# Low parts of split weights: a ScalarE copy and an accumulating DMA in place of a VectorE subtraction

## The chip, the cores and the metric

The kernel runs on one core of one Trainium2 chip. The metric is the device time of one execution in microseconds, as the median of the runs; the profile is one execution with its instructions recorded.

## The reference

The reference takes 512 tokens of 1024 features through one hybrid block (a selective state-space branch, a gated linear recurrence, retention and RWKV-7, merged by gates, then a gated feed-forward with a short convolution) and through two layers of a second block (three kinds of attention merged by gates, a feed-forward, a per-layer embedding). All of it is float32. Most of the work is in products of activations with weights, of this kind:

```
proj   = h @ w_in                      # [512, 1024] @ [1024, n]
branch = einsum('bsmw,mwd->bsmd', ys, w_branch)
x      = x + (silu(gate) * value) @ w_down
```

## The kernel before, in words

Activations lie with features on the 128 partitions and the 512 tokens along the free dimension. A product makes one chunk of 128 output features at a time. Its weights come as one tile of 128 partitions by 1024 columns (eight blocks of 128 input features; some have 768, 512, 256 or 128 columns).

TensorE multiplies in a fast format that keeps some 12 bits of an operand. So each operand is held as two parts, high and low, whose sum is the float32 value, and each block of a product is three matmuls: high by high, high weights by low activations, low weights by high activations (`mm3`, L226). `wtile` (L218) brings one weight tile in and splits it: SyncE loads the float32 weights into a tile `wr` (pool of NWR = 3 buffers), ScalarE rounds them into `whi` (3 buffers), and VectorE subtracts `whi` from `wr` into `wlo` (2 buffers). The helper `act` (L164, the instruction at L166) is the ScalarE copy, `tt` (L175, L176) the VectorE subtraction, `dma` (L169, L170) the load on SyncE's queue, `mm` (L172, L173) the matmul. `pmm` (L233) runs the three matmuls of each block into one PSUM tile `pj` (2 buffers), 24 matmuls for a tile of eight blocks. `proj` (L242) is one tile load and its `pmm`. Nearly all weight tiles go through `proj`; values and embeddings call `wtile` themselves (L995, L1197, L1741), and so do the compressed keys and values of attention (`compress`, L1436; its wtile at L1451), whose tiles feed only eight short matmuls each, and which stand between projections of full length.

The program calls `wtile` 579 times. The framework orders the instructions of each engine ahead of time and puts semaphores between engines; an engine works its own list strictly in order. A tile's buffer is written again once the last reader of the tile that held it is done. So the copy into `whi` of one tile waits for the last matmul of the tile three before it, and the load into `wr` waits for the subtraction of the tile three before it. GpSimd has hardly anything to do: it clears tiles and takes the power -0.5 of a few columns for the norms (`rsqrt`, L246, the instruction at L251). No DMA is issued on its queue.

The stages, by time from the start of the span: the RWKV projections and the recurrence up to about 400 us, the state-space and retention branches with the RWKV inverse to about 800, the RWKV scan woven with the branch products to about 1230, the feed-forward to about 1650, then two layers of attention (each some 550 us, with `compress` in the first 50) and feed-forward (each some 450 us).

Of the kernel before, what the change touches and what calls it, by code (L numbers as in the profile page):

```python
# [11 lines left out]
F32R = mybir.dt.float32r  # L12
# [7 lines left out]
P = 128  # L20
# [7 lines left out]
NWR = 3  # L28
# [10 lines left out]
def _param_layout():  # L39
    """Columns of the packed per-feature parameters: name -> (first column, columns)."""  # L40
    sizes = [
        ("norm_mix", 8), ("ssm_conv_w", 64), ("ssm_conv_b", 16), ("ssm_norm", 8), ("ssm_d", 8),
        ("lru_conv_w", 32), ("lru_conv_b", 8), ("lru_b_a", 8), ("lru_b_i", 8), ("lru_lam", 8),
        ("ret_norm", 8), ("rwkv_mu", 26), ("rwkv_w0", 8), ("rwkv_a0", 8), ("rwkv_k_k", 8),
        ("rwkv_k_a", 8), ("rwkv_r_k", 8), ("rwkv_ln_w", 8), ("rwkv_ln_b", 8), ("norm_ffn", 8),
        ("ffn_conv_w", 132), ("ffn_conv_b", 44), ("norm_final", 8),
        ("mix_norm_2", 16), ("ffn_norm_2", 16), ("ple_norm_2", 16), ("c_q_norm_2", 4),
        ("c_kv_norm_2", 4), ("final_norm_2", 8),
    ]
    out, c = {}, 0  # L50
    for n, w in sizes:
        out[n] = (c, w)
        c += w
    return out, c
# [3 lines left out]
# constants that depend on shapes alone: name -> (first column, columns)  # L58
# [15 lines left out]
class Unit:  # L74
    """Softmax attention of 128 queries over T sets of n keys that share a bank of scores."""
# [65 lines left out]
class B:  # L141
    """The parts of the program share these helpers, pools and constants."""
# [66 lines left out]
    def split(self, hi, lo, src, scale=None):  # L209
        """hi + lo == src (times a per-feature column), each part exact in the fast format."""  # L210
# [7 lines left out]
    def wtile(self, src, n=1024):  # L218
        raw = self.wr.tile([P, 1024], F32, tag="wr", name=self.name("wr"))
        self.dma(raw[:, :n], src)  # L220
        hi = self.wh.tile([P, 1024], F32R, tag="whi", name=self.name("whi"))
        lo = self.wh.tile([P, 1024], F32R, tag="wlo", name=self.name("wlo"), bufs=2)
        self.split(hi[:, :n], lo[:, :n], raw[:, :n])
        return hi, lo

    def mm3(self, out, ws, xs, first, last):  # L226
        """out += (wh + wl)^T (xh + xl) without the product of the two low parts."""
# [5 lines left out]
    def pmm(self, w, off, x, kc, m=P):  # L233
        """One chunk of m output features from the split weights w, from column off on."""
# [7 lines left out]
    def proj(self, src, x, kc=KC, m=P):  # L242
        """One chunk of m output features: src is [128, kc * m] of DRAM, x the split activations."""
        return self.pmm(self.wtile(src, kc * m), 0, x, kc, m)

    def rsqrt(self, out, ss, scale, eps):  # L246
        """out = (ss * scale + eps) ** -0.5 on a few columns."""
# [5 lines left out]
    def col_sums(self, out, xs):  # L253
        """out[:, t]: sums of the columns of all xs, tokens on partitions."""
# [6 lines left out]
    def rstd_rows(self, sq, dst, n=D):  # L261
        """sq: [128, S] (or several), whose column sums are sums of squares; dst[:, t] = rsqrt(mean + eps)."""
# [6 lines left out]
    def bcast_cols(self, r, dst):  # L269
        """The columns r [128, 4] of tokens as one row [., S] on every partition."""  # L270
# [9 lines left out]
    def softplus_neg_abs(self, out, ax, tmp):  # L280
        """out = log1p(exp(-ax)) for ax >= 0, by 2 atanh(e / (2 + e))."""
# [24 lines left out]
    def block1_consts(self):  # L306
# [23 lines left out]
        # 4 * softplus(-lam)  # L330
# [14 lines left out]
    def first_norm(self):  # L345
        """h = rms_norm(x) in two parts, features on partitions."""
# [28 lines left out]
    # -- RWKV --  # L375
    def rwkv_setup(self, pool):
# [11 lines left out]
        # w2: high parts on the lower half of the partitions, low parts on the upper; a2 the other way round  # L388
# [12 lines left out]
    def mix(self, pool, ps, ch, tag, bufs):  # L401
        """Token shift: x (1 - mu) + previous x mu."""
# [5 lines left out]
    def rwkv_lora(self, pool):  # L408
        """Chunks 24 (wl | al) and 25 (gl) of the mixed projection."""
# [20 lines left out]
    def lora(self, i, cs):  # L430
        """The second product of decay (0) or rate (1): (high + low) high, then high low."""
# [13 lines left out]
    def rwkv_core(self, pool, p):  # L445
# [6 lines left out]
        # decay  # L452
# [11 lines left out]
        # a  # L464
# [5 lines left out]
        # normalised key direction  # L470
# [19 lines left out]
        # bonus  # L490
# [6 lines left out]
        # values, tokens of a chunk on partitions, the two heads stacked  # L497
# [57 lines left out]
    def swap_halves(self, dst, src):  # L555
        """dst[(h, t), c, v] = src[(h, v), (c, t)] for halves h of the partitions and chunks c of 64."""
# [9 lines left out]
    def rwkv_inverse(self, pool):  # L566
        """(I + A)^-1 of every head and chunk, A strictly upper triangular: forward substitution in the two
        diagonal blocks of 32, one problem a partition, then the block above them by matrix products."""
# [25 lines left out]
        # four problems on the partitions: -X11 (A12 X22), with A12 and then (X11 A12)^T on block diagonals  # L594
# [60 lines left out]
    def rwkv_step(self, pool, p, c, st, ld, bank):  # L655
        """One chunk of the recurrence over the states of a pair of heads."""
# [32 lines left out]
    def rwkv_scan(self, pool, p, y):  # L689
        """The recurrence of a pair of heads, its norm and output."""  # L690
# [38 lines left out]
    # -- RG-LRU --  # L729
    def conv4(self, pool, ps, w, n, ch, b, tag, bufs=2, taps=4):  # L730
        """Causal depthwise convolution along the tokens of [128, S]."""
# [47 lines left out]
    # -- Mamba-2 --  # L779
    def silu_gate(self, pool, ps, tag, tmp, bufs=1):  # L780
        """silu(ps) = (1 + tanh(x / 2)) x / 2."""
# [7 lines left out]
    def ssm_setup(self, pool, tmp):  # L789
        """dt, its cumulative sums about each block's middle, and what follows from them."""  # L790
# [38 lines left out]
        # from the block's start, and about its middle  # L829
# [7 lines left out]
        # dt exp(end - cum)  # L837
# [112 lines left out]
    # -- retention --  # L950
    def rope(self, pool, ps, cos, sin, half, rows, tag, bufs=1, tmp=(("ropr", 1), ("rops", 1))):
        """x cos + swap(x) sin, halves of each head swapped across partitions by DMA."""
# [12 lines left out]
    def stack(self, pool, src, e, tag, bufs=1):  # L965
        """[high; low] parts of head e stacked on the partitions."""
# [6 lines left out]
    def dup(self, pool, src, e, tag, bufs=1):  # L973
        """The high part of head e on both halves of the partitions, and the low part."""
# [9 lines left out]
    def ret_pair(self, pool, j, y):  # L984
# [7 lines left out]
        # values with tokens on partitions  # L992
# [54 lines left out]
    def finish_ret(self):  # L1047
        """The last steps of the heads whose norms were begun one stage before."""
# [8 lines left out]
    # -- gates, branch products, merge --  # L1057
# [4 lines left out]
    def gates1(self, pool):  # L1062
        """tanh(gate / 2) of the four branches, chunk by chunk."""
# [7 lines left out]
    def branch(self, pool, m, y, gates, norm=None):  # L1071
        """merged (+)= (1 + tanh(gate / 2)) * (y_m W_m): twice the gated sum."""
# [20 lines left out]
    def norm_in(self, pool, c, x, w, acc, tag="nsq", bufs=2, gain=1.0):  # L1093
        """Chunk c of x (times gain) joins the sum of squares; its product with w is split into h."""
# [11 lines left out]
    def new_row(self):  # L1106
        """The row of 1 / rms by which products with h are still to be multiplied."""
# [6 lines left out]
    def out_proj(self, pool, w, m, xres, gain, g0, tag="xr", bufs=4, due=None):  # L1114
        """x += m w; the new x goes to DRAM, its normalised form to h. due: a row and gains still missing in x."""
# [15 lines left out]
    def ffn(self, up, down, conv, pool, done, mid=None, late=None):  # L1131
        """x + W_down (silu(gate) value); done(j, x_j) takes each finished chunk."""
# [51 lines left out]
    def embeddings(self, pool, i, tags=None):  # L1184
        """The per-layer embeddings p W of layer i, to DRAM."""
# [22 lines left out]
    def mid_norm(self, pool, fill):  # L1208
        """Block 1's last norm and block 2's first: x still lacks the first one's gain and row1, h the row of both."""
# [19 lines left out]
    def block1(self):  # L1229
# [10 lines left out]
        def weave(main, fill, ratio):  # L1240
            """One step of `fill` after every `ratio` steps of `main`; then what is left of fill."""
# [99 lines left out]
    def rope_tables(self, tmp):  # L1341
        """cos and signed sin of positions x frequencies, the angle reduced to [-pi, pi]."""
# [38 lines left out]
    def rope_load(self, pool, n, row):  # L1381
        """The rotary tables, times the row of 1 / rms if that is still due."""
# [18 lines left out]
    def rope2(self, pool, pt, cs, half, tag="ra", bufs=2):  # L1401
        """x cos + swap(x) sin, halves of each head swapped across partitions by DMA."""
# [16 lines left out]
    def to_tokens(self, pool, src, tag, rows=P, n=P, bufs=1):  # L1419
        """[rows, S] features x tokens to [128 tokens, 4, n]."""  # L1420
# [8 lines left out]
    def compress(self, pool, i, src, kv, out):  # L1429
        """gelu((blocks + pos) w1): leaves the hidden activations' transpose [128, 2, 64] in out."""  # L1430
# [15 lines left out]
        for t in range(4):  # L1446
            # high parts in columns 0 to 63 of each product's stationary operand, low parts in the others
# [24 lines left out]
    def attn_a_setup(self, pool, i):  # L1472
        """Projections of branch A: queries, its three kinds of keys and values, gates."""
# [24 lines left out]
        # selected and window keys side by side, high parts and low parts on both halves  # L1498
# [14 lines left out]
        # compressed keys on both halves of the partitions, one block of columns a head of a pair  # L1513
# [11 lines left out]
        # compressed values, one copy for each head of the group on its own rows and columns  # L1525
# [33 lines left out]
    def units(self, seq):  # L1559
        """Attention units in stages, each unit's transposes and products behind later units' scores."""  # L1560
# [24 lines left out]
    def o_chunk(self, oN, o, c):  # L1585
        """Features 128 c.. of the outputs back to features on partitions, split."""
# [5 lines left out]
    def attn_a(self, pool, o):  # L1592
        """Compressed, selected (every block is among the selected) and window attention."""
# [72 lines left out]
    def attn_b(self, pool, i, o):  # L1666
        """Sliding window of a block of queries over its own and the previous block, with sinks."""
# [27 lines left out]
    def attn_c_setup(self, pool, i):  # L1695
        """Normalised low-rank queries and keys, and the shared rotary key."""
# [38 lines left out]
    def attn_c(self, pool, i, o):  # L1735
        """Latent attention: 64 plain and 32 rotary features a head."""
# [3 lines left out]
        # values, tokens on partitions  # L1740
# [9 lines left out]
        # the rotary key is the same for every head  # L1750
# [48 lines left out]
    def gates2(self, pool, i):  # L1799
        """tanh(gate / 2) of the three branches, chunk by chunk."""  # L1800
# [8 lines left out]
    def branch2(self, pool, i, m, o, gates):  # L1809
        """merged (+)= (1 + tanh(gate / 2)) (o W): twice the gated sum."""  # L1810
# [19 lines left out]
    def weave(self, main, fill, ratio):  # L1830
        """One step of fill after every `ratio` steps of main."""
# [7 lines left out]
    def layer2(self, i, last):  # L1839
# [31 lines left out]
        with tc.tile_pool(name="ff2", bufs=1, reuse_waits="tile") as pool:  # L1871
# [11 lines left out]
            # per-layer embedding  # L1883
# [33 lines left out]
def _ahead(gs):  # L1917
    """The items of gs, each handed out once the next one has been prepared."""
# [188 lines left out]
```

## Time and profile before

| what | value |
|---|---|
| median of 3 runs | 3707.62 us (3706.73 to 3713.56) |
| span of the profiled execution, first to last instruction | 3707.9 us |
| instructions | 47402 |
| granted TensorE clock, mean over the span | 0.988 |

The profile gives no other time of that execution than its span; the span lies 0.3 us above the median and within the spread of the runs, so differences are counted against 3707.9 us and put on the median unchanged. "Busy" counts a TensorE matmul from its start to a modelled end. Consecutive matmuls overlap, so the step from one start to the next is shorter than one matmul's busy time. PEld is the loading of the stationary operand, beside the matmuls.

### The profile page before, as it was taken

What the parts mean: (1) busy time and instruction counts of PE and PEld (TensorE: products, weight loads), DVE (VectorE), ACT (ScalarE), POOL (GpSimd) and SP (SyncE); (2) the same over time, 40 slices, a digit from 0 to 9 for tenths busy, and PEclk for the clock granted to TensorE, in tenths of its full rate; (3) what the DMA queues carried; (4) which work ended last, traced back from release to release, by engine and by line L of the source; (5) the groups of instructions that cost most, each with busy time, mean ns of one, the idle gap of its engine ahead of it and who ended that gap; (6) DMA issues with size and microseconds to landing.
All of it is one profiled execution on the core that took longest, in us unless ns stands there. A gap on an engine that the chain in (4) does not pass through costs nothing.

```text
span 3707.9 us, 47402 instructions
## 1 busy us (share of the span) xinstructions
PE 3630.3 (98%) x17806; PEld 2953.0 (80%) x17806; DVE 2328.7 (63%) x4416; ACT 1543.6 (42%) x2619; POOL 53.2 (1%) x61
## 2 busy tenths in 40 slices
PE   8999999999999999999999999999999999999998
PEld 6887788877878788877888787888778887878886
DVE  6777897654454586657776655544677766554445
ACT  5665533323233353344555533222445655432223
POOL 0000000000000000000000000000000000000000
PEclk9999999999999999999999899999999999999999
DMA  5443545355543532344222124233442221343332
GB/s 182 141 135 116 154 123 142 107 152 161 158 132 108 162 108 91 103 135 150 76 66 68 58 82 154 92 96 95 139 134 80 64 69 55 102 141 96 95 93 97
DMA packets 230388, 417.86 MB, mean 113 GB/s; under 512 B 99632, under 2 KB 105648, under 8 KB 230032
## 3 DMA queue, kind: packets, MB, share of 16 engines
q1 hardware_dynamic: 230160, 414.84, 36.3%
q8 instruction: 141, 2.31, 0.3%
q14 instruction: 87, 0.71, 0.1%
HBM read 349.81 MB, written 55.38 MB: 109 GB/s over the span
## 4 chain that ended last, share of the span: by engine, by line
PE 66%; DVE 2%; ACT 1%; issue 0%; DMA 0%; POOL 0%; SPq 0%; POOLq 0%; DVEq 0%; ACTq 0%
PE pj L173 56%; PE ps L173 4%; PE pl L173 4%; PE ps L119 2%; DVE wlo L176 0%; DVE cc L176 0%; PE ps L1589 0%; POOL r L251 0%; ACT PT L166 0%; DVE ro L176 0%; ACT qf L166 0%; ACT P L167 0%; DVE kd L176 0%; DVE qf L176 0%; DVE xa L193 0%
## 5 line engine op out<-in xcount | busy, mean ns | idle before, releaser
L173 PE MATMUL pj<-hhi,whi 128*128 128x512 f32 (+1 forms) x2824 | 1137.6, 403 | 6.4 <-DVE scv L193 2.1
L173 PE MATMUL pj<-hhi,wlo 128*128 128x512 f32 (+1 forms) x2824 | 1127.2, 399 | 5.9 <-DVE wlo L176 5.8
L173 PE MATMUL pj<-hlo,whi 128*128 128x512 f32 (+1 forms) x2824 | 1128.0, 399 | 0.0
L166 ACT ACTIVATE whi<-wr 128x1024 fp32r<-128x1024 f32 (+3 forms) x579 | 573.4, 990 | 1289.1 <-PE pj L173 1140.3
L176 DVE TENSOR_TENSOR wlo<-wr,whi 128x1024 fp32r<-128x1024 f32 (+3 forms) x579 | 654.8, 1131 | 165.1 <-PE pj L173 104.2
L173 PEld LDWEIGHTS pj<-hhi,wlo 128*128 128x128 f32 (+1 forms) x2824 | 531.4, 188 | 135.9 <-DVE wlo L176 10.3
L173 PEld LDWEIGHTS pj<-hhi,whi 128*128 128x128 f32 (+1 forms) x2824 | 532.1, 188 | 130.8 <-issue 3.3
L173 PEld LDWEIGHTS pj<-hlo,whi 128*128 128x128 f32 (+1 forms) x2824 | 532.2, 188 | 122.8 <-issue 4.5
L173 PE MATMUL pj<-gl,whi 128*128 128x512 f32 x528 | 208.6, 395 | 0.0
L173 PE MATMUL pj<-gh,wlo 128*128 128x512 f32 x528 | 208.6, 395 | 0.0
L173 PE MATMUL pj<-gh,whi 128*128 128x512 f32 x528 | 208.5, 395 | 0.0
L176 DVE TENSOR_TENSOR fg<-pj,row 128x512 f32<-128x512 f32 x82 | 56.7, 691 | 212.7 <-PE pj L173 212.6
L176 DVE TENSOR_TENSOR xa<-pj,xa 128x512 f32<-128x512 f32 x72 | 49.8, 692 | 193.5 <-PE pj L173 193.3
L167 ACT ACTIVATE P<-ps,a 128x256 f32<-128x256 f32 (+3 forms) x256 | 128.3, 504 | 53.8 <-DVE a L189 49.9
L173 PE MATMUL pj<-o,whi 128*128 128x512 f32 x384 | 132.5, 421 | 0.0
L173 PE MATMUL pj<-yh,whi 128*128 128x512 f32 x320 | 131.1, 410 | 1.4 <-ACT yh L166 1.4
L173 PE MATMUL pj<-yl,whi 128*128 128x512 f32 x320 | 129.4, 404 | 0.5 <-DVE yl L176 0.5
L173 PE MATMUL pj<-yh,wlo 128*128 128x512 f32 x320 | 128.9, 403 | 0.0
L166 ACT ACTIVATE PT<-ps 128x256 f32<-128x256 f32 (+3 forms) x200 | 98.3, 492 | 71.0 <-PE ps L119 56.9
L173 PEld LDWEIGHTS pj<-gl,whi 128*128 128x128 f32 x528 | 99.0, 187 | 24.3
L173 PEld LDWEIGHTS pj<-gh,whi 128*128 128x128 f32 x528 | 99.0, 187 | 24.2
L173 PEld LDWEIGHTS pj<-gh,wlo 128*128 128x128 f32 x528 | 99.0, 187 | 24.2
(504 smaller groups left out, 5209.9 us busy)
## 6 DMA issues: line engine op xcount, KB each, us to landing
wr<-in_ffn_up SPq DMA_DIRECT2D x132, 512.0 KB, 3.4
wr<-in_w_in SPq DMA_DIRECT2D x122, 512.0 KB, 3.7
wr<-in_ffn_down SPq DMA_DIRECT2D x48, 512.0 KB, 3.5
wr<-in_w_bg SPq DMA_DIRECT2D x48, 512.0 KB, 3.4
wr<-in_w_gate SPq DMA_DIRECT2D x32, 512.0 KB, 3.5
wr<-in_w_branch SPq DMA_DIRECT2D x32, 512.0 KB, 3.5
wr<-in_w_out SPq DMA_DIRECT2D x24, 512.0 KB, 3.5
wr<-in_w_br SPq DMA_DIRECT2D x48, 256.0 KB, 2.6
```

Source lines behind the costliest of these rows:

```text
L119: b.nc.tensor.transpose(pt[:, k * P:(k + 1) * P], self.P[:, k * P:(k + 1) * P], b.ident)
L166: return self.nc.scalar.activation(out, in_, f, bias=bias, scale=scale)
L167: return self.nc.scalar.activation(out, in_, f, bias=bias, scale=scale, accum_out=accum)
L173: return self.nc.tensor.matmul(out, lhsT, rhs, start=start, stop=stop)
L176: return self.nc.vector.tensor_tensor(out, a, b, op=op)
```

## The change

In `wtile` the split is written out anew. ScalarE writes minus the rounded weights into `wlo` (a copy with scale -1) and then the rounded weights into `whi` as before. A DMA issued on GpSimd's queue then reads the same weights from DRAM a second time and adds them onto `wlo` in place, so that `wlo` ends as weights minus rounded weights. VectorE has no part in it. The raw tile `wr` has 2 buffers in place of 3, `wlo` has 3 in place of 2, `whi` still has 3. The other lines of the diff take out docstrings and comments and leave the instructions as they are; line numbers stay.

```diff
-NWR = 3
+NWR = 2
...
     def wtile(self, src, n=1024):
         raw = self.wr.tile([P, 1024], F32, tag="wr", name=self.name("wr"))
         self.dma(raw[:, :n], src)
-        hi = self.wh.tile([P, 1024], F32R, tag="whi", name=self.name("whi"))
-        lo = self.wh.tile([P, 1024], F32R, tag="wlo", name=self.name("wlo"), bufs=2)
-        self.split(hi[:, :n], lo[:, :n], raw[:, :n])
+        hi = self.wh.tile([P, 1024], F32R, tag="whi", name=self.name("whi"), bufs=3)
+        lo = self.wh.tile([P, 1024], F32R, tag="wlo", name=self.name("wlo"), bufs=3)
+        self.act(lo[:, :n], raw[:, :n], AF.Copy, scale=-1.0)
+        self.act(hi[:, :n], raw[:, :n], AF.Copy)
+        self.nc.gpsimd.dma_start(lo[:, :n], src, accum_op=ALU.add)
         return hi, lo
```

## Rows read from the trace of the kernel before

**Rows 1.** The page, part 1: busy time, share of the span, instructions.
```profile
PE 3630.3 (98%) x17806; PEld 2953.0 (80%) x17806; DVE 2328.7 (63%) x4416; ACT 1543.6 (42%) x2619; POOL 53.2 (1%) x61
```

**Rows 2.** Waits of TensorE: engine, tile, line, waited for, total us, times, longest.
```profile
PE pj L173 <- ACT whi L166: 10.2, 3, 8.6
PE ps L173 <- DVE dg L176: 7.6, 10, 2.1
PE pj L173 <- DVE wlo L176: 5.8, 7, 1.5
PE ps L173 <- DVE Z L176: 5.7, 5, 2.9
PE ps L173 <- DVE hl L176: 5.4, 2, 3.6
```

**Rows 3.** Windows: PE, PEld, DVE, ACT, POOL busy, clock, DMA share, GB/s.
```profile
2300.00:2600.00 300.00, 300.00 (x1288) 241.51 (x1287) 135.65 (x165) 78.60 (x92) 0.00 (x0) 1.00 0.30 93
1250.00:1650.00 400.00, 399.67 (x1715) 320.29 (x1715) 275.46 (x375) 164.50 (x206) 1.44 (x4) 1.00 0.36 115
400.00:600.00 200.00, 196.87 (x1074) 163.32 (x1074) 172.43 (x336) 83.17 (x118) 5.95 (x5) 0.99 0.55 143
```

**Rows 4.** Groups by shape: copies and subtractions of weight tiles.
```profile
L166 ACT ACTIVATE whi<-wr 128x1024 fp32r<-128x1024 f32 x484 | 512.9, 1060 | 1078.0 <-PE pj L173 953.9 <-issue 97.8 <-DMA wr<-in_w_in 10.2
L176 DVE TENSOR_TENSOR wlo<-wr,whi 128x1024 fp32r<-128x1024 f32 x484 | 589.2, 1218 | 153.9 <-PE pj L173 101.5 <-issue 43.8 <-DMA zb_kr<-s_KR 4.6
L166 ACT ACTIVATE whi<-wr 128x512 fp32r<-128x512 f32 x50 | 31.5, 631 | 101.0 <-PE pj L173 94.8 <-issue 4.5 <-ACT kd L166 1.5
```

**Rows 5.** Timeline of the first feed-forward: start us, us, engine, line.
```profile
1407.65 1.06 ACT L166 ACTIVATE whi<-wr 128x1024 fp32r<-128x1024 f32 x1 [1.37 <-PE pj L173]
1407.69 0.39 PE L173 MATMUL pj<-hhi,whi 128*128 128x512 f32 x1
1407.92 0.39 PE L173 MATMUL pj<-hlo,whi 128*128 128x512 f32 x1
...
1413.25 1.06 ACT L166 ACTIVATE whi<-wr 128x1024 fp32r<-128x1024 f32 x1 [3.31 <-PE pj L173]
...
1418.89 0.39 PE L173 MATMUL pj<-hhi,whi 128*128 128x512 f32 x1
1419.36 0.39 PE L173 MATMUL pj<-hhi,wlo 128*128 128x512 f32 x1
```

**Rows 6.** DMA issues: KB each, median us to landing; and the queue.
```profile
q1 hardware_dynamic: 230160, 414.84, 36.3%
...
wr<-in_ffn_up SPq DMA_DIRECT2D x132, 512.0 KB, 3.4
wr<-in_w_br SPq DMA_DIRECT2D x48, 256.0 KB, 2.6
```

**Rows 7.** GpSimd's groups: the norm's power, the longest clearing.
```profile
L251 POOL TENSOR_TENSOR r<-rs,mhalf 128x4 f32<-128x4 f32 x15 | 16.2, 1078 | 2584.1 <-DVE rs L190 2584.1
L600 POOL MEMSET invbd<- 128x2048 f32 x1 | 1.8, 1814 | 57.1 <-DVE invt L176 57.1
```

**Rows 8.** Timeline of the compressed keys, first layer of attention.
```profile
1710.10 1.06 ACT L166 ACTIVATE whi<-wr 128x1024 fp32r<-128x1024 f32 x1 [2.00 <-PE pj L173]
...
1717.43 0.28 PE L173 MATMUL ps<-wlo,hl 128*128 128x256 f32 x1
```

**Rows 9.** Timeline of the last branch product, first layer of attention.
```profile
2195.94 0.63 ACT L166 ACTIVATE whi<-wr 128x512 fp32r<-128x512 f32 x1 [4.92 <-PE pj L173]
...
2202.07 0.40 PE L173 MATMUL pj<-o,wlo 128*128 128x512 f32 x1
```

**Rows 10.** Timeline of the start: the first weight tile.
```profile
7.51 1.06 ACT L166 ACTIVATE whi<-wr 128x1024 fp32r<-128x1024 f32 x1 [0.92 <-DMA wr<-in_w_pp]
9.88 0.80 PE L173 MATMUL pj<-ph,wlo 128*128 128x512 f32 x1
```

**Rows 11.** The tile wr: its load's issue on SyncE, minimum, median, maximum ns.
```profile
L170 SPq DMA_DIRECT2D wr<-in_ffn_up x132: 327/328/333, 1255.5 to 3537.0; - x132
```

**Rows 12.** The line L190: a VectorE tensor-scalar of 512 columns.
```profile
L190 DVE TENSOR_SCALAR a<-a x8: 419/421/428, 64.0 to 373.8; 128x512 f32<-128x512 f32 x8
```

## The prediction

> **What bounds the kernel now.** I read the busy shares first, then TensorE's waits, then the windows by stage, then one weight tile in the timeline. TensorE is busy 98% of the span, 3630.3 of 3707.9 us; VectorE is at 63%, ScalarE at 42%, GpSimd at 1% [rows 1]. So taking work off VectorE can give back at most the 77.6 us in which TensorE idles, and of that only what VectorE ends. TensorE's waits are short and spread: the five largest are 10.2, 7.6, 5.8, 5.7 and 5.4 us in total, and only one, 5.8 us, names the subtraction that goes away [rows 2]. In the feed-forward of the second block TensorE never idles: 1288 matmuls in 300 us, one per 0.233 us, while VectorE is busy less than half of the time [rows 3]. There the kernel is TensorE's pace and nothing else.
>
> What the change can lose depends on how early a weight tile is split. In the feed-forward the copies into whi start at 1407.65 and 1413.25, one per 5.60 us, each when TensorE starts a new tile (1407.69), that is, when the last matmul of the tile three before has let the buffer go. The tile copied at 1407.65 is the one that TensorE starts two tiles later, at 1418.89, and its low part is first needed by the third matmul, at 1419.36 [rows 5]. So from the release of a buffer to the first use of the low part there are 11.7 us in a stage of full tiles: two tiles of 5.6 us and two matmuls. I call this the lead.
>
> **The change, part by part.**
>
> *Removed:* 579 subtractions on VectorE, of which the 484 full ones take 1.218 us each, 589.2 us [rows 4]. VectorE isn't the bound, so this lies beside TensorE. What is on the path is the wait for wlo, 5.8 us [rows 2]; it goes, and so may a part of the other VectorE-ended waits (7.6 + 5.7 + 5.4 us), which are mostly latency, not queueing. I take -8 us, with bounds 0 and -25 us (all four rows).
>
> *Added on ScalarE:* a second copy per tile, 1.06 us for a full one and 0.63 us for 512 columns, in all again what the copies into whi take, 512.9 + 31.5 us and a little [rows 4]. ScalarE was at 42% and goes to some 57%. Most of its idle time ahead of these copies is spent waiting for TensorE (953.9 us), so the second copy fits. The high part now comes 1.06 us later; it has 11.2 us. Copies and evacuations queued behind it on ScalarE come up to 1.06 us later. Where such work ends a wait of TensorE, this may cost; I take +3 us, bounds 0 and +12.
>
> *The raw tile* has two buffers. It comes free after the second copy of the tile two before, so the load is issued 2.1 us after that copy's start; it lands 3.4 us after issue [rows 6], and is due 11.2 us after that copy's start. Cover of 5.7 us hides it; nothing.
>
> *The accumulating DMA* is the term that decides. Its chain starts when the wlo buffer comes free: the copy into wlo (1.06 us [rows 4]), the issue on GpSimd, the transfer, then the matmul. No row shows a DMA issued by GpSimd. For the issue the nearest rows are SyncE's own, 0.33 us [rows 11], and GpSimd's longest instruction, 1.81 us; I take 1.0 us, as of a short GpSimd instruction (1.08 us) [rows 7]. For the transfer, the lower end is the plain load of the same 512 KB, 3.4 us to landing [rows 6]. The upper end is three such passes, reading the weights, reading wlo and writing wlo, one after the other: 10.2 us. I take two passes, 6.8 us, because read and write of a plain load overlap already and what is new is the second read. With 0.15 us for semaphores the chain is 1.06 + 1.0 + 6.8 + 0.15 = 9.0 us, against a lead of 11.7 us. So full tiles are covered with 2.7 us to spare, 0 us. At the upper end it is 12.4 us or more, and every full tile is late. With three buffers, three tiles then take one chain plus one tile's own time, (12.4 + 5.6) / 3 = 6.0 us a tile in place of 5.6.
>
> Where tiles are short the lead is shorter:
> - Compressed keys and values: the tile copied at 1710.10 is needed at 1717.43, a lead of 7.3 us [rows 8]. There are 16 such tiles, each late by 9.0 - 7.3 = 1.7 us: +27 us.
> - The last branch products: 6.1 us of lead [rows 9] against 0.63 + 1.0 + 2 x 2.6 (a 256 KB load, [rows 6]) + 0.15 = 7.0 us; some 5 tiles in each of two layers, 0.9 us each, +9 us, and the first full tile behind them 2.5 us late in each layer, +5 us.
> - The start: the first low part is there at 7.51 + 9.0 = 16.5 us in place of 9.88 [rows 10], +7 us.
>
> *GpSimd's queue:* the 15 powers of the norms [rows 7] now stand among 579 DMA issues. Each may wait for one issue of 1.0 us; half of them on the path, +7 us.
>
> Sum: -8 + 3 + 27 + 14 + 7 + 7 = +50 us, 3707.9 + 50 = 3758 us. The span is 0.3 us over the median, so it stands for the median.
>
> One rule of the Trainium skill weighs on the issue. Rows show that VectorE runs tensor-scalar instructions of 0.42 us on float32 [rows 12]; no row shows GpSimd writing descriptors beside them. The Trainium skill, "SBUF — State Buffer", section "Who interferes with whom", says that while VectorE runs in a two-port mode GpSimd can't write descriptors, and advises against DMAs from GpSimd beside it. By that rule the issue would be up to 0.42 us longer when it meets such an instruction; on the 27 or so short tiles above that would add about 11 us, 3769 us in place of 3758.
>
> **The rivals.**
>
> *A, the accumulation binds.* The 16 DMA engines are busy 0.30 of the time at 93 GB/s in the pure feed-forward, 0.36 in the first one and 0.55 between 400 and 600 us [rows 3]. That is one pass of the weights per tile. Two more make 0.90 and 0.96, still under 1; three more make 1.20, and the engines become the pace. Its place is the feed-forwards, its point of decision where one accumulated tile costs more than about 2.3 loads. Weight loads are some 280 MB of the 414.84 MB that fill 36.3% of the span [rows 6]; at 93 GB/s per 0.30 they are 903 us of the engines' time. All DMA, 0.363 x 3707.9 = 1346 us, plus three times 903 us makes 4055 us; with stages that don't balance, up to 4200. If the chain alone is late (12.4 us), 0.4 us on some 500 full tiles gives 3950 us. For it: nothing in the profile prices a read-modify-write. Against: the shares now are low. The Trainium skill, "DMA: Bandwidth & Descriptors", section "Issuing engines are not separate DMA queues", says that transfers of every issuing engine run on the same 16 DMA engines and interleave; by that rule a GpSimd queue gives no room of its own and this sum holds, and no run here shows it yet. Chance 0.27, 3950 to 4200 us.
>
> *B, it is hidden entirely.* If the transfer is little dearer than a load, the chain is 1.06 + 0.5 + 3.4 + 0.15 = 5.1 us, under every lead above but the start's. Then +3 us at the start, +7 us of GpSimd's queue at most, and -8: within 0.2% of now, 3705 to 3714 us. Chance 0.14.
>
> *C, faster.* As B, and VectorE's relief is worth the whole 25 us of its waits: 3683 to 3700 us. For it: VectorE is busy 172 of 200 us between 400 and 600 [rows 3]. Against: TensorE is busy 196.87 us of the same stretch. Chance 0.14.
>
> That the change doesn't do what it says has no room: without the second DMA the low parts would be wrong.
>
> **How the numbers follow.** A measurement of this kernel tells a change from none at about 0.2%, 7.4 us. The forecast, a chain between 6.5 and 11.5 us, gives +15 to +110 us, 3722 to 3818 us, and has 0.45. Slower: 0.45 + 0.27 = 0.72; same 0.14; faster 0.14. The range reaches down to 3692, leaving out the lower half of C, and up to 4200, leaving out the last of A, where a pass costs more than I bounded.
>
> **What would show it.** VectorE's share should fall to some 45%, ScalarE's rise to 57%. The accumulating DMAs should land 6 to 8 us after issue, the feed-forward windows keep 1288 matmuls in 300 us with a DMA share near 0.9, and waits of TensorE for the landing of wlo should stand at the compressed keys, the last branch products and the start. Fewer matmuls in the feed-forward windows make me wrong towards A; landings under 4.5 us and no such waits make me wrong towards B or C.

## The result, and the profile after

The changed kernel takes 3876.32 us (median of 4 runs, 3869.61 to 3887.61), the kernel before 3707.18 us beside it (4 runs, 3703.66 to 3713.56). The ratio is 1.0456, with a 95% interval of 1.0437 to 1.0476: 169 us slower. The forecast was 50 us slower, 3758 us, in a range of 3692 to 4200 us. The sign holds, the size doesn't.

The profiled execution took 3887.61 us, with a span of 3885.9 us, 178.0 us above the span of before. The differences of time below are between these two spans, unless medians are named.

The busy time by engine, which answers to [rows 1], and then the span and the mean granted clock of the core (0.988 before):

```profile
PE 3686.3 (95%) x17806; PEld 2984.5 (77%) x17806; DVE 1761.7 (45%) x3837; ACT 2027.2 (52%) x3200; POOL 557.5 (14%) x640
```
```profile
core 0: 3885.9 us, clock 0.975
```

The same 17806 matmuls take 56.0 us more of TensorE's time, and TensorE idles 199.6 us where it idled 77.6 us. The two differences, 56.0 and 122.0 us, are the 178.0 us. Most of the first is clock: a mean of 0.975 over 3885.9 us leaves 97.1 us of full-speed time out, and 0.988 over 3707.9 us leaves 44.5 us out, 52.6 us less. Some of that falls on time in which TensorE idles; counted where it is busy, the low clock takes 49 us more than before.

TensorE's waits, the answer to [rows 2]: what it waited for, total us, times, longest.

```profile
PE pj L173 <- DMA wlo<-in_w_in: 49.5, 17, 5.3
PE ps L173 <- DVE acc L176: 14.8, 4, 4.4
PE pj L173 <- DMA wlo<-in_w_pp: 12.2, 3, 6.0
PE pj L173 <- ACT whi L166: 11.9, 3, 9.9
PE pj L173 <- DVE xr L176: 8.4, 7, 2.3
PE pj L173 <- DMA wlo<-in_w_out: 6.7, 3, 2.7
...
PE pj L173 <- DMA wlo<-in_w_rv: 5.8, 3, 2.3
```

All waits for the landing of a low part, the four groups shown and smaller ones of other weights, come to 90.5 us. Before, waits for VectorE's subtraction came to 6.7 us. So 84 of the 122 us of new idle time name the accumulating DMA. Of the other 38 us most name VectorE: its other waits rose from some 32 to 61 us. Loads that aren't weights are named for 7 us.

The windows of the changed kernel, with the columns of [rows 3]: the feed-forward, the stage of the scan and the branch products behind it, the compressed keys of the first layer.

```profile
2450.00:2700.00 250.00, 250.00 (x1073) 200.79 (x1072) 67.34 (x98) 110.33 (x125) 38.42 (x44) 1.00 0.90 191
840.00:1420.00 580.00, 547.88 (x2560) 440.32 (x2559) 200.78 (x436) 249.12 (x370) 83.30 (x88) 0.97 0.88 208
1740.00:1860.00 120.00, 94.75 (x401) 71.83 (x400) 44.87 (x92) 60.03 (x84) 19.65 (x23) 0.91 0.90 223
```

In the feed-forward TensorE doesn't idle and keeps its pace, 1073 matmuls in 250 us (0.233 us each), though the DMA engines are at 0.90. In the scan stage it idles 32 of 580 us; the window of before that does nearly the same work (2478 matmuls against 2560) shows less, 10 of 530 us:

```profile
800.00:1330.00 530.00, 520.45 (x2478) 420.26 (x2478) 275.04 (x489) 170.90 (x280) 14.56 (x12) 0.99 0.48 144
```

To place the loss, I compared the start of the n-th matmul in both traces. Both issue the same 17806, in an order that differs in places: 14575 positions hold the same matmul, and the others are shifted among their neighbours, by less than 25 us. So a step is good to a stage, not to a tile. The difference grows by 18 us in the first 140 us of before, by 26 us between 370 and 700 us, by 36 us between 818 and 1326 us (scan, branch products, output projection) and by 5 us just behind that, early in the first feed-forward. It grows by 26 and 32 us at the compressed keys of the two layers of attention, by 6 and 2 us just behind them, and by 16 and 14 us at the last branch products and output projections. Elsewhere it falls by 4 us in all, and the rest of the feed-forwards adds 0.5.

The DMA issues after, KB each and median us to landing, the answer to [rows 6], with the queues:

```profile
q0 software_dynamic: 83376, 279.02, 41.0%
q1 hardware_dynamic: 230160, 414.84, 36.6%
...
wr<-in_ffn_up SPq DMA_DIRECT2D x132, 512.0 KB, 6.4
wlo<-in_ffn_up POOLq DMA_DIRECT2D x132, 512.0 KB, 7.6
wr<-in_w_in SPq DMA_DIRECT2D x122, 512.0 KB, 5.6
wlo<-in_w_in POOLq DMA_DIRECT2D x122, 512.0 KB, 7.2
...
yraw<-y SPq DMA_DIRECT2D x32, 256.0 KB, 6.4
...
zb_kr<-s_KR SPq DMA_DIRECT2D x32, 128.0 KB, 6.6
xr<-xs SPq DMA_DIRECT2D x16, 256.0 KB, 4.8
```

And the same loads before:

```profile
wr<-in_w_in SPq DMA_DIRECT2D x122, 512.0 KB, 3.7
...
yraw<-y SPq DMA_DIRECT2D x32, 256.0 KB, 4.0
zb_kr<-s_KR SPq DMA_DIRECT2D x32, 128.0 KB, 3.4
xr<-xs SPq DMA_DIRECT2D x16, 256.0 KB, 2.8
```

The accumulating transfer lands in 7.6 and 7.2 us in the two largest groups; the medians of all groups of 512 KB lie between 5.9 and 8.1 us. What the prediction doesn't have is the other half of the view: these loads on SyncE's queue, the same transfers as before, land 1.5 to 2 times as late, 6.4 against 3.4 us for wr in the feed-forward [rows 6].

One tile of the compressed keys in the timeline (start us, us, engine, line), the answer to [rows 8]:

```profile
1778.48 0.53 SPq L170 DMA_DIRECT2D wr<-in_w_in  x1
...
1782.93 0.80 PE L173 MATMUL pj<-hhi,wlo 128*128 128x512 f32 x1 [3.41 <-DMA wlo<-in_w_in]
...
1785.62 1.06 ACT L166 ACTIVATE wlo<-wr 128x1024 fp32r<-128x1024 f32 x1 [5.06 <-DMA wr<-in_w_in]
...
1785.66 0.63 PE L173 MATMUL pj<-hhi,wlo 128*128 128x512 f32 x1
...
1786.97 0.86 POOL L227 DMA_DIRECT2D wlo<-in_w_in  x1 [7.68 <-ACT wlo L166]
...
1788.05 0.39 PE L173 MATMUL pj<-hhi,wlo 128*128 128x512 f32 x1
...
1793.83 0.50 PE L173 MATMUL pj<-hhi,wlo 128*128 128x512 f32 x1 [1.88 <-DMA wlo<-in_w_in]
```

The raw load is issued at 1778.48 and ends ScalarE's wait at 1785.62, 7.1 us later, with two accumulations issued just ahead of it (1777.18 and 1778.43). Copy, issue and accumulation follow, and TensorE gets the low part at 1793.83. The whole chain is 15.4 us. The prediction's chain began at the copy.

The same stretch in three windows of 4 us (columns as above) shows what a stall does to the clock:

```profile
1779.00:1783.00 4.00, 0.46 (x2) 0.26 (x2) 1.80 (x3) 1.54 (x4) 0.29 (x1) 0.75 0.91 201
1783.00:1787.00 4.00, 4.00 (x10) 3.13 (x11) 1.99 (x3) 1.38 (x2) 0.03 (x1) 0.50 1.01 256
1788.00:1792.00 4.00, 3.94 (x21) 3.08 (x20) 1.38 (x3) 1.61 (x2) 0.00 (x0) 1.00 0.88 169
```

TensorE is idle for most of the first 4 us. In the next 4 the granted clock is 0.50, the 1.2 GHz level, and matmuls of 512 columns start 0.43 us apart. From 1788 it is 1.00, 2.4 GHz, and they start 0.23 us apart. (The count of 21 there is no measure: eight of them have 256 columns.) Ten matmuls at 0.43 us in place of 0.23 are 2 us, paid on top of the stall of 3.41 us.

### The profile page after: what moved, and what is told of

The parts are those of the page before. It is cut to its first block, busy times and chain, and to the rows that moved or that the text cites. A ratio compares the mean times of both kernels' runs of the same rounds, so it can differ in the third digit from the quotient of the medians.

```text
span 3885.9 us, 48672 instructions
## 1 busy us (share of the span) xinstructions
PE 3686.3 (95%) x17806; PEld 2984.5 (77%) x17806; DVE 1761.7 (45%) x3837; ACT 2027.2 (52%) x3200; POOL 557.5 (14%) x640
## 4 chain that ended last, share of the span: by engine, by line
PE 42%; DMA 6%; issue 3%; ACT 1%; DVE 1%; POOL 0%; SPq 0%; POOLq 0%; DVEq 0%; ACTq 0%
PE pj L173 34%; PE ps L173 3%; PE pl L173 3%; DMA wlo<-in_w_in 3%; DMA xr<-xs 2%; PE ps L119 1%; DMA rb<-ro 0%; POOL wlo L227 0%; DMA wlo<-in_w_bg 0%; DMA wlo<-in_w_out 0%; DMA wlo<-in_w_br 0%; DVE xr L176 0%; SPq L170 0%; PE ps L1593 0%; ACT wlo L166 0%
## 5 line engine op out<-in xcount | busy, mean ns | idle before, releaser
L173 PE MATMUL pj<-hhi,wlo 128*128 128x512 f32 (+1 forms) x2824 | 1142.2, 405 | 59.4 <-DMA wlo<-in_w_in 49.5
L166 ACT ACTIVATE wlo<-wr 128x1024 fp32r<-128x1024 f32 (+3 forms) x579 | 565.7, 977 | 83.5 <-PE pj L173 31.0
L227 POOL DMA_DIRECT2D wlo<-in_w_in x122 | 107.0, 877 | 797.1 <-ACT wlo L166 714.8
L227 POOL DMA_DIRECT2D wlo<-in_ffn_up x132 | 115.0, 871 | 642.2 <-ACT wlo L166 642.2
```

The source lines that it names most:

```text
L166: return self.nc.scalar.activation(out, in_, f, bias=bias, scale=scale)
L173: return self.nc.tensor.matmul(out, lhsT, rhs, start=start, stop=stop)
L227: self.nc.gpsimd.dma_start(lo[:, :n], src, accum_op=ALU.add)
```

## The experiments

Four theories stood against each other. **L** (lead): low parts arrive late where the lead is short, so TensorE waits for the chain itself. **D** (DMA load): the accumulations fill the DMA engines, and other loads land late. **O** (order): the new order of instructions costs the time, whatever the transfer does. **S** (ScalarE): the second copy and the changed buffers cost it. Ratios are to the kernel before on the same chip (medians 3703.57, 3707.32 and 3706.93 us in three groups of runs), with 95% intervals.

**VectorE adds in place of the DMA.** Copies and buffers of the changed kernel stay.

```diff
-        self.nc.gpsimd.dma_start(lo[:, :n], src, accum_op=ALU.add)
+        self.tt(lo[:, :n], raw[:, :n], lo[:, :n].bitcast(F32), ALU.add)
```

> The changed kernel, but VectorE adds the weights onto the negated copy (one tensor-tensor add per tile) and GpSimd issues no DMA; the second ScalarE copy and the buffers (2 raw, 3 high, 3 low) stay. Theory L (low parts land late, and TensorE's clock drops behind the stalls) and theory D (the DMA engines are so busy that other loads come late) both expect 3700 to 3730 us, the time of the kernel before within 0.6%. Theory S (the second ScalarE copy and the two raw buffers hold up other work) expects 3800 us or more.

3704.12 us, 0.9998 [0.9989, 1.0008]. The second copy on ScalarE and the buffers together cost nothing that can be measured, and S falls. All of the loss comes with the DMA.

**A plain load in place of the accumulation.** It overwrites the low part with the weights, so another product is computed; engine, issue and bytes read from HBM stay.

```diff
-        self.nc.gpsimd.dma_start(lo[:, :n], src, accum_op=ALU.add)
+        self.nc.gpsimd.dma_start(lo[:, :n], src)
```

> The changed kernel, but the GpSimd DMA overwrites the low tile with the weights instead of accumulating onto it, so the products take the weights themselves as low parts; queue, waits and bytes read from DRAM are the same, the second read of the tile is gone. Theory L expects the landing time to fall from 7.2-7.6 us to about 4 us and the time to 3720 to 3770 us. Theory D expects the DMA share to fall from 0.77 to about 0.6 and the same time. Theory O (the instructions stand in another order because the low tile is filled by a DMA) expects no fall in the time: 3850 us or more.

3754.08 us, 1.0137 [1.0117, 1.0157]: 50 us slower than before, not 169. Every engine executes its instructions in the changed kernel's order. The DMA queues and issues of this kernel:

```profile
q0 software_dynamic: 83376, 279.02, 22.3%
...
wr<-in_ffn_up SPq DMA_DIRECT2D x132, 512.0 KB, 3.5
wlo<-in_ffn_up POOLq DMA_DIRECT2D x132, 512.0 KB, 4.5
wr<-in_w_in SPq DMA_DIRECT2D x122, 512.0 KB, 4.2
wlo<-in_w_in POOLq DMA_DIRECT2D x122, 512.0 KB, 4.7
```

GpSimd's queue takes 22.3% of 3755.5 us here, 837 us of the engines' time, against 41.0% of 3885.9, 1593 us, with the accumulation: a ratio of 1.90 for the same packets and MB. That is the "two passes" of the prediction, measured as the engines' time; by the landing, 7.6 against 4.5 us, the ratio is 1.7. Raw loads land in 3.5 us again in the feed-forward and in 4.2 us for w_in (3.4 and 3.7 before), and TensorE's waits for low parts fall from 90.5 to 35.6 us. O can hold at most these 50 us, which the extra load itself has to share; some 120 us are the accumulation.

**Where the loss sits: by stage.** In the next four kernels, and in the last one of this section, a switch chooses the way for each tile; they differ in where it is set (in the second of them it is turned round).

```diff
+        if self.acc:
             self.act(lo[:, :n], raw[:, :n], AF.Copy, scale=-1.0)
             self.act(hi[:, :n], raw[:, :n], AF.Copy)
             self.nc.gpsimd.dma_start(lo[:, :n], src, accum_op=ALU.add)
+        else:
+            self.split(hi[:, :n], lo[:, :n], raw[:, :n])
```

Accumulation in the feed-forwards alone (204 tiles):

> Accumulating DMA for the 204 weight tiles of the three feed-forwards alone, VectorE's subtraction for the other 375; buffers as in the changed kernel. Theory L expects almost nothing lost, since there the lead is 11.7 us and the chain about 10 us: 3700 to 3725 us, VectorE's wait at the start and at the compressed keys as before. Theory D expects 3720 to 3760 us, as the transfers at the ends of the feed-forwards come late. Theory S expects a loss in proportion to the tiles, 204 of 579 of 169 us, 3765 us.

3712.39 us, 1.0023 [1.0013, 1.0032]. Everywhere but there (375 tiles):

> The complement: accumulating DMA for the 375 tiles outside the feed-forwards, VectorE's subtraction in the feed-forwards. Theory L and theory D both expect nearly the whole loss, 3850 to 3880 us. Theory S expects 3815 us.

3860.56 us, 1.0423 [1.0399, 1.0447]. The two losses, 9 and 157 us, add to 166 of the 169 us. So the stage in which the DMA engines are busiest for longest pays almost nothing: its 11.7 us of lead [rows 5] cover the chain, copy, issue and landing, of 1.06 + 0.87 + 7.6 us.

**The setup of attention back on VectorE**, which is where the compressed keys are made:

```diff
+            self.acc = False
             drain(self.attn_a_setup(pool, i))
+            self.acc = True
```

> The changed kernel, with VectorE's subtraction for the tiles of the setup of attention in both layers (compressed keys and values and the projections between them), the accumulating DMA everywhere else. Theory L (late low parts where the lead is short, each stall followed by a drop of TensorE's clock) expects the loss of that stretch back, 26 + 32 us by the two traces, so 3815 to 3830 us. Theory D (transfers come late in all of the kernel because the DMA engines are busy) expects at most the share of the traffic that goes, some 10% of 169 us: 3855 to 3870 us.

3821.88 us, 1.0321 [1.0292, 1.035]: 54 us back, as L said. By the n-th matmul, the steps of 26 and 32 us that end at matmuls 8400 and 13200 become -1 us each. The run takes chain and traffic out of the stretch together. In the changed kernel TensorE's waits for low parts are 20 us there in the first layer, the line below (1740 to 1860 us), and 19.5 us in the second (2820 to 2960 us).

```profile
PE pj L173 <- DMA wlo<-in_w_in: 19.9, 7, 4.6
```

**The scan, its branch products and the output projection back on VectorE:**

```diff
+                self.acc = False
                 self.rwkv_scan_setup(pool)
...
             self.out_proj(bp, self.ap["w_out"], (mh, ml), self.ap["xT"], "norm_ffn", 0, "gth", NG1)
+            self.acc = True
```

> The changed kernel, with VectorE's subtraction from the RWKV scan to the end of the first output projection, the accumulating DMA everywhere else. In that stretch TensorE waits only 7 us for low parts in the changed kernel, but the stretch is some 45 us longer than before. Theory D (there the loads of the scan, and what VectorE and ScalarE do with them, come late behind the accumulating traffic) expects 3825 to 3840 us. Theory L alone expects 3860 to 3870 us.

3850.49 us, 1.0395 [1.0378, 1.0412]: 26 us back by the medians, 46 by the spans, between the two expectations. The stretch itself goes from +36 to +2 us by the n-th matmul, and what else moved between these traces doesn't belong to it. In the changed kernel, between 840 and 1420 us, the waits of all engines for loads include these:

```profile
DVE xr L176 <- DMA xr<-in_xT: 25.5, 6, 8.4
ACT yh L166 <- DMA yraw<-y: 18.4, 9, 4.3
...
PE ps L173 <- DMA zb_kr<-s_KR: 6.7, 5, 2.0
...
PE pj L173 <- DMA wlo<-in_w_gate: 5.0, 2, 4.5
...
PE pj L173 <- DMA wlo<-in_w_branch: 1.5, 2, 1.0
```

TensorE's own waits for low parts are 6.5 us here (the last two lines). The others are for loads that the change doesn't touch, and before they were nearly absent: 0.2 us for xr and 4.0 us for yraw between 800 and 1330 us, none of TensorE for zb_kr. A wait of 8.4 us for xr is more than its median landing explains, 4.5 us against 3.3 before; what else delays it was not followed. With VectorE in this stretch, the two loads of the scan come back to where they were:

```profile
yraw<-y SPq DMA_DIRECT2D x32, 256.0 KB, 4.2
zb_kr<-s_KR SPq DMA_DIRECT2D x32, 128.0 KB, 3.5
```

So here the loss is mostly D by the trace; the medians alone don't decide it. The run takes both out here, too; the next one has the traffic alone.

**Traffic that nobody waits for.** The kernel before, with two raw buffers, and on GpSimd an accumulation of half of each tile into a scratch tile that is never read.

```diff
...
+        self.nd = 1 - self.nd
+        d = self.dummy[:, self.nd]
+        self.nc.gpsimd.tensor_copy(d[:, 0:1], hi[:, 0:1].bitcast(F32))
+        self.nc.gpsimd.dma_start(d[:, :n // 2], src[:, :n // 2], accum_op=ALU.add)
```

> The kernel before with two raw buffers, plus an accumulating DMA per weight tile that reads half of the tile's weights and adds them onto a scratch tile that nobody reads; it is held back by a one-column GpSimd copy of the high part, so that it starts when the changed kernel's would. Theory L (late low parts) expects 3700 to 3725 us, since nobody waits for it. Theory D (the DMA engines are too busy for the other loads) expects about half of the loss, 3760 to 3800 us.

3791.86 us, 1.0225 [1.0208, 1.0242]. Its base is the kernel before with the two raw buffers and nothing else:

```diff
-NWR = 3
+NWR = 2
```

> The kernel before with two raw buffers in place of three, the base of e5_idle_half (3791.9 us), whose difference to it is the idle traffic alone. If the buffers cost nothing, 3700 to 3715 us, and the idle half traffic costs about 84 us. If the two buffers cost much of it, 3740 us or more.

3721.63 us, 1.0047 [1.0031, 1.0064], between the two expectations: the two raw buffers cost 15 us of it, and the traffic and its issue 70 us. No matmul reads what these DMAs write, and the subtraction is VectorE's. The one-column copy reads the high part and could hold up its buffer; ScalarE waits for it for 1.6 us in all here. The issues of the kernel with the idle traffic:

```profile
q0 software_dynamic: 83376, 139.53, 22.9%
...
wr<-in_w_in SPq DMA_DIRECT2D x122, 512.0 KB, 4.4
...
yraw<-y SPq DMA_DIRECT2D x32, 256.0 KB, 5.2
...
zb_kr<-s_KR SPq DMA_DIRECT2D x32, 128.0 KB, 5.0
```

22.9% is 870 us of the engines' time, near that of the plain reload, and the loads of the scan are again late, 5.2 us (yraw) and 5.0 us (zb_kr) against 3.8 and 3.2 us in its base. D is real, and worth tens of us without any wait for an accumulated low part. It also shows by stage: by the n-th matmul, half the bytes with nobody waiting add 16 us in the stretch of the scan (its base 0), 14 us between 370 and 700 us (base 2), and 14 and 10 us at the compressed keys (base 4 and 6). So the traffic alone has a share of the loss at the compressed keys too.

**The whole of it idle, outside the feed-forwards**, as two halves:

```diff
...
+        for e in range(0 if self.acc else 2):
+            d, m = self.dummy[:, e], n // 2
+            self.nc.gpsimd.tensor_copy(d[:, 0:1], hi[:, 0:1].bitcast(F32))
+            self.nc.gpsimd.dma_start(d[:, :m], src[:, e * m:(e + 1) * m], accum_op=ALU.add)
...
```

> As e5_idle_half, but all the bytes, in two halves, and only for the 375 tiles outside the feed-forwards: the same accumulating traffic as e4_all_but_ffn (3860.6 us), with nobody waiting for it. Theory L expects 3700 to 3735 us. Theory D expects 3830 to 3870 us. A value between shares the loss between the two.

3998.93 us, 1.0786 [1.0765, 1.0807], dearer than the change itself. This run measures something else; its waits say what (L169 is the ScalarE copy here, three lines further down):

```profile
ACT whi L169 <- POOL dummy L229: 296.7, 68, 8.1
```

GpSimd fell behind on the scratch halves, and its one-column copy held the high buffers, so ScalarE waited 296.7 us for it. The run is inconclusive for D.

**Three raw and two high buffers** in the changed kernel, to take the raw load out of the chain:

```diff
-NWR = 2
+NWR = 3
...
-        hi = self.wh.tile([P, 1024], F32R, tag="whi", name=self.name("whi"), bufs=3)
+        hi = self.wh.tile([P, 1024], F32R, tag="whi", name=self.name("whi"), bufs=2)
```

> The changed kernel with three raw buffers and two high ones in place of two and three. Theory L with the raw load as a link of the chain (it now lands 5.6 to 6.4 us after issue and starts only when the copies of the tile two before are done) expects 3820 to 3855 us. Theory L without that link, and theory D, expect no fall: 3865 to 3900 us.

3861.37 us, 1.0415 [1.04, 1.0431], 15 us less than the changed kernel and short of what the raw load as a link would give. The waits moved more than they went: TensorE's for wlo of w_in fell from 49.5 to 29.0 us, but those for wlo of cmp_w rose from 2.4 to 15.7 us, and those for the high part from 11.9 to 18.2 us. With one high buffer fewer this doesn't separate the link.

**Four low and two high buffers**, to lengthen the lead:

```diff
-        hi = self.wh.tile([P, 1024], F32R, tag="whi", name=self.name("whi"), bufs=3)
-        lo = self.wh.tile([P, 1024], F32R, tag="wlo", name=self.name("wlo"), bufs=3)
+        hi = self.wh.tile([P, 1024], F32R, tag="whi", name=self.name("whi"), bufs=2)
+        lo = self.wh.tile([P, 1024], F32R, tag="wlo", name=self.name("wlo"), bufs=4)
```

> The changed kernel with four low buffers and two high ones. Theory L with the release of the low buffer as the start of the chain expects a lead longer by one tile everywhere and 3780 to 3840 us. Theory L with the raw load as the link that decides, and theory D, expect no fall: 3865 to 3900 us.

4559.98 us, 1.2303 [1.2282, 1.2323], a miss by every theory. Waits of ScalarE and TensorE in it:

```profile
ACT wlo L166 <- DMA wr<-in_ffn_up: 607.2, 122, 8.0
...
PE pj L173 <- ACT whi L166: 360.9, 188, 10.4
```

With two high buffers the raw tile stays held until a high buffer is free, the next raw load starts late, and ScalarE's copy into wlo, first in its queue, waits for that load while TensorE waits for the high part behind it. That is read from these two lines and not tested further. The lead in low tiles is not tested by this run.

**Accumulation only where leads are long**: the feed-forwards and the tiles woven with attention.

```diff
+            self.acc = True
             oa = self.new_o(pool)
...
             drain(fill)
+            self.acc = False
             drain(self.branch2(pool, i, 2, oc, gates))
```

> The accumulating DMA in the feed-forwards and for the tiles woven with attention alone, where leads are long and the DMA engines are least busy; VectorE's subtraction elsewhere. Theories L and D both expect 3700 to 3715 us, no measurable difference to the kernel before or a trace of a loss. Well under 3700 us would mean that relief of VectorE is worth something where it runs beside attention.

3718.09 us, 1.0034 [1.0022, 1.0046], 3 us above what both theories expected. Even there it gains nothing over the kernel before. No version here beats it.

## Why the prediction was right in sign and wrong in size

**Right: the bound, and that VectorE's relief is worth little.** VectorE fell to 45% as forecast and nothing came of it. ScalarE rose to 52%, not 57%: by the span 483.6 us were added, though the 579 copies sum to 565.8 us, as a copy right behind another starts before that one ends (1777.09 and 1778.04 us, 1.05 us long). The +3 us for the second copy can't be told from 0 in the run with VectorE's add, whose interval reaches from -4 to +3 us. Rival C, with VectorE's waits worth 25 us, has nothing for it. Nor has the -8 us of the sum: the 6.7 us for the subtraction went, but all waits of TensorE that name VectorE rose from 39 to 61 us.

**Right: the price of one accumulation.** Two passes, 6.8 us, were taken; 7.2 and 7.6 us were measured to landing in the two largest groups, and 1.90 times the engines' time of a plain load. The issue was taken at 1.0 us; the instructions of the tile wlo on GpSimd (minimum, median, maximum ns) give 0.87 us:

```profile
L227 POOL DMA_DIRECT2D wlo<-in_ffn_up x132: 862/872/924, 1341.3 to 3725.8; - x132
L227 POOL DMA_DIRECT2D wlo<-in_w_in x122: 862/872/1213, 26.5 to 2996.8; - x122
```

The prediction weighed a rule on descriptors held up by VectorE's two-port modes (the Trainium skill, "SBUF — State Buffer", section "Who interferes with whom") at up to 0.42 us an issue. Over 254 issues here the maximum is 0.34 us above the median and the median is 10 ns above the minimum: nothing of that size shows as a rule of this kernel, though a rare issue can be of that kind.

**Right: rivals A and B.** The feed-forward keeps its pace at a DMA share of 0.90, the forecast number, so the accumulation doesn't bind as a stream, and A falls. The waits for low parts that B excludes are there: 18 us in the first 160 us, 39 us at the compressed keys of both layers, and 10 us at the last branch products and output projections. So B falls.

**The norms' powers cost little, less than was taken.** They were given +7 us for 15 powers. There are 31: rows 7 show the largest of three groups. The power itself takes 1.03 us (1.08 us before; its line is L255 now, as lines behind `wtile` stand four further down). VectorE's waits for the three are 39 us where they were 33, and VectorE isn't the bound; what reaches TensorE of these 6 us no run shows.

**Wrong: "The raw tile has two buffers ... Cover of 5.7 us hides it; nothing."** The cover was worked out for full tiles of the feed-forward, with the 3.4 us landing of before. There it holds: 2.1 + 6.4 us is under 11.2 us. At the compressed keys the same load took 7.1 us behind accumulations of other tiles, inside the chain, which is 15.4 us and not 9.0 us. Forecast there +27 us; measured 58 us by the two steps of the n-th matmul, and 54 us by the run that puts VectorE back. The late tiles aren't the ones that were counted, either: nearly all of these waits name w_in, the full tiles that stand between the compressed ones, and only 2.4 us name the compressed tiles. The trace of before had a sign of it, a copy of w_in in this stretch that waits for its raw load:

```profile
1705.84 1.06 ACT L166 ACTIVATE whi<-wr 128x1024 fp32r<-128x1024 f32 x1 [1.94 <-DMA wr<-in_w_in]
```

Over the compressed keys of the first layer ScalarE's copies wait 5 us for raw loads before (1641 to 1746 us) and 15 us after (1727 to 1860 us). The start went the same way, 18 us for 7 us. The last branch products with the output projections lost 16 + 14 us for 14 us, but the waits for low parts there are 10 us, under the forecast; the rest of that loss was not taken apart. That the raw load is the link is seen in the timeline; the run meant to remove it changed the high buffers too and didn't settle how much it is worth.

**Wrong: a term that isn't there.** The prediction counted DMA engines for rival A, as capacity, and gave the delay of other loads no price. The rows above show it: yraw, zb_kr, xr from xs and the raw tiles land 1.5 to 2 times as late. The stretch from 818 to 1326 us, forecast at nothing, loses 36 us with 6.5 us of waits for low parts. The idle half traffic alone costs 16 us in it and 70 us in all. The Trainium skill, "DMA: Bandwidth & Descriptors", section "Issuing engines are not separate DMA queues", says that transfers of all issuing engines interleave on the same 16 DMA engines. The trace agrees: accumulations on GpSimd's queue took SyncE's 512 KB load in the feed-forward from 3.4 to 6.4 us. Plain loads on the same queue, at a DMA share of 0.59 between 2450 and 2700 us in place of 0.90, left it at 3.5 us, so a second queue alone doesn't do it. The prediction cited this rule for the pace of a stream, and it should have been read for the latency of every other load.

**Wrong: idle time counted once.** Each new stall was priced at its length. The 122 us of new idle time came with 56 us of slower matmuls, as in the three windows above. The idle time alone is 122 us; most of the 56 us, 49 us, is the lower clock.

**Open.** The loss between 370 and 700 us, 26 us, was not split between L and D by a run of its own; the idle half traffic adds 14 us there, so D has a part in it. The shares of L and D at the compressed keys, and the rise in waits that name VectorE, were not taken apart. Of the 50 us that the plain reload loses, neither the order nor the extra load was measured by itself. That clock could be won back with stalls in place wasn't tried.

## What to carry to other kernels

Price an accumulating DMA at about two passes of the DMA engines, and then price what those passes do to the landing of every load that some stage waits for. A lead is worth what the shortest stage has, counted from the issue of the first load in the chain, not from the copy in the middle of it. To each new stall of TensorE add what the granted clock takes behind it: here 49 us of lower clock on 122 us of idle time.

## What was not expected of the hardware

- An accumulating DMA of 512 KB took 1.90 times the DMA engines' time of a plain one with the same packets and bytes, and landed in 7.2 and 7.6 us against 4.7 and 4.5 us in the two largest groups.
- GpSimd's issue of it takes 0.87 us; that of the plain load 0.54 us, as its group in the plain-load kernel shows (total busy us, mean ns, then idle time before it):

```profile
L227 POOL DMA_DIRECT2D wlo<-in_ffn_up x132 | 70.9, 537 | 669.4 <-ACT wlo L166 669.4
```

- DMA engines at 0.90 of their time hardly touched TensorE's pace in the feed-forwards, 5 us early in the first one and 0.5 us over the rest of all three, while the stage of the scan lost 36 us at about the same share (0.88). The share alone doesn't say what a stage loses.
